# Reordering the products of an MLP's up stage, and preparing two attention weights one stage earlier

## The chip, the core and the metric

The kernel runs on one core of a Trainium2 chip. The metric is the device time of one execution in microseconds (us), and the time of a kernel is the median of its runs. Three runs of the kernel before are known: 2131.23, 2133.43 and 2618.16 us, median 2133.43 us. One more execution was taken with the hardware profiler; it took 2129.71 us.

## What is computed

A two-layer decoder trunk on 1024 tokens of width 1024, in float32:

```python
h = x @ conv_w_in + b;  h = a * sigmoid(gate);  h = depthwise_conv31(h)     # layer 0, token mixer
y = silu(layer_norm(h)) @ conv_w_out + b
...
q = rope(x @ attn_w_q);  k = rope(x @ kv_w_k);  v = x @ kv_w_v               # layer 1, token mixer
y = softmax_with_sink(q k^T in a window of 128) v @ attn_w_o
...
x = layer_norm(ALPHA * x + y)                                               # then, in both layers:
x = layer_norm(ALPHA * x + square(relu(x @ w_up)) @ w_down)                 # MLP, inner width 4096
x = x + (p @ ple_w_proj) * sigmoid(x @ ple_w_gate)                          # gate
```

`w_q` and `w_o` are 1024 x 1024, `w_up` and `w_down` 1024 x 4096 and 4096 x 1024.

## The kernel before, in words

**Three products for one.** Every float32 operand of a matmul is split into a high part, rounded to the fast format, and a low part, the rest. ScalarE (ACT) writes the high part with a cast, VectorE (DVE) the low part with a subtraction (`split`), and TensorE (PE) adds high x high, high x low and low x high (`mm3`). A 128-row step of a 512-column product is thus three matmuls.

**Low parts made ahead.** For some weights the low part is made one stage early, written to DRAM and only loaded when it is needed. `unit_ahead` does this for one unit of `w_q` or `w_o`, a tile of 128 x 1024. For each of its two halves it loads 128 x 512 (256 KB) into a tile with a given tag, casts it into a second tile of that tag, subtracts, and stores the low half to DRAM (`low_half`). That is two loads, two casts, two subtractions and two stores for a unit. `w_q` has eight units, `w_o` is given four here. The consumer later loads the weight itself and its low part with `prep(ap, low=...)`. `work(what, k, tag)` is the call that records one unit, with a priority 400 places later than its place in the program (`LOW_BY`).

**The up stage** (`mlp`, lines 1335 to 1426) takes the 32 column blocks of `w_up` in 16 pairs, f = 0, 2, ..., 30. Each pair is computed as a 2 x 2 block product with seven products in place of eight; a product here is 12 matmuls of 128 x 512. `top_left(f)` makes two of them, into one bank of PSUM and a second one, and its sum gives the first result c11. Then come the products with the four token forms T[2], T[3], T[1] and T[4], and one with the plain tokens `plain[1, 1]`. The running bank p of `top_left` takes T[2], is copied by ACT (c21), takes T[1], is copied (c22), takes `plain[1, 1]` and becomes c12. A second bank r takes T[3] and then T[4]; it is added to c22 between the two and to c21 after T[4]. For the five pairs in `EARLY` = 0, 2, 4, 6, 8 `top_left` runs ahead of the loop. `keep` sums and stores the results. The weights come through a stream `ws` of five slots in the order in which `ws.add` is given them.

**The down stage** (`down_seven`) goes through the eight blocks of the inner width in five groups, `DOWN` = (0), (1, 2), (3, 4), (5, 6), (7). A group makes seven products. In a group of two blocks a product is 48 matmuls into four banks; DVE adds each bank to the output x. The forms of the operands alternate between quarters of the token buffers. In the third group the residual is added as well: 16 loads and 16 DVE operations (`residual`). `product` notes the last matmul ahead of its own as `mark`; the residual loads may start after it (`nc.after(mark)`).

**The gate and the attention.** `ple(0)` computes the gate of layer 0. After its sixth set of products it records eight `work` units for `w_q`, with tag X. Then `attention` makes keys and values (the KV part, with `w_kv`); at the first of its two token groups it records four units for `w_o`, with tag X. The queries follow.

**What sets the order.** A recording layer (`Recorder`) notes every operation, and `schedule` lays them out on the engines with a list scheduler: on each engine the operation that is ready goes first, the smaller priority first, by costs that are written into `cost`. `nc.slack` adds a time in ns to the moment at which the operations recorded under it count as ready: `WORK_SLACK` 1000, `UP_SLACK` 2000. The order is fixed when the program is built; on the chip each engine and the DMA queue of SyncE (SP) run theirs strictly one after the other. All loads and stores are issued by SP. All operations carry line 479, where the recorded calls are made, so the rows of the profile are told apart by tile names: X and z are tags of general tiles, `ps` and `tr` are banks of PSUM, `xh`/`xl` are token buffers or forms, `wh`/`wl` weight slots, `t`, `g`, `bo`, A, B and E general tiles.

Of the kernel before, what the change touches and what calls it, by code (L numbers as in the profile page):

```python
# [16 lines left out]
T = 1024  # L17
# [46 lines left out]
EARLY = 0, 2, 4, 6, 8  # L64
# [4 lines left out]
WORK_SLACK = 1000.0  # L69
UP_SLACK = 2000.0  # L70
# [441 lines left out]
class Emit:  # L512
# [822 lines left out]
    def mlp(self, i):  # L1335
        nc, d, ws = self.nc, self.d, self.ws
        tags, xtags = (dict(zip((2, 1, 3, 4), "XAEB")), "EB") if i == 0 else (dict(zip((2, 1, 3, 4), "XEAB")), "AB")
        pairs = list(range(0, NFF, 2))
        units = {}
        for f in pairs:  # L1340
            u = self.low.get((i, f)) or self.pair_units([d["w_up"][i, f + k] for k in range(2)], f in EARLY)
            units[f] = u if len(u) == 4 else u + self.pair_units([d["w_up"][i, f + k] for k in range(2)], True)[1:]
        ws.add(*[units[f][0] for f in EARLY])
        for f in pairs:
            ws.add(*units[f][f in EARLY :])

        plain = {
            (a, h): [self.xs(k + 4 * a, h * HT, HT) for k in range(4)]
            for a, h in ((0, 0), (1, 0), (1, 1))
        }  # L1350

        def prod(u, half, B, ps=None):
            wh, wl = u
            o = half * HT
            more = ps is not None
            ps = ps if more else self.ps()
            self.mm3(ps, [
                (wh[:, o + k * P : o + (k + 1) * P], wl[:, o + k * P : o + (k + 1) * P], *B[k]) for k in range(4)
            ], not more, True, more)
            return ps  # L1360

        def copy(ps, tag="t"):
            v = self.sb(tag)
            nc.scalar.copy(v, ps)
            return v

        def plus(a, ps):
            nc.vector.tensor_tensor(out=a, in0=a, in1=ps, op=ALU.add)
            return a

        def top_left(f):
            w = ws.get(1)[0]
            p = prod(w, 0, plain[0, 0])
            c = copy(p)
            p2 = prod(w, 1, plain[1, 0])
            ws.done(1)
            return p, self.square(plus(c, p2))

        for k in range(3):
            nc.move("tr", "ps")  # L1380
        banks = {}
        for f in EARLY:
            banks[f], c = top_left(f)
            self.store(i, f, (0, 0), c)
        T = self.token_forms(tags)
        self.quiet = nc.tile("xh01", (P, 4, HT), F32), nc.tile("xl01", (P, 4, HT), F32R)
        self.seven_forms(f"gate{i}", 4)
        self.seven_forms(f"down{i}", 2)

        for f in pairs:  # L1390
            early = f in banks
            if early:
                p, c11 = banks[f], self.sb("t")
                o = f % 4 // 2 * HT
                nc.sync.dma_start(c11, self.hid[i][f // 4, (0, 0)][:, o : o + HT])
            else:
                p, c11 = top_left(f)
            w12 = ws.get(1)[0]
            prod(w12, 0, T[2], p)
            c21 = copy(p)  # L1400
            w34 = ws.get(1)[0]
            r = prod(w34, 0, T[3])
            prod(w12, 1, T[1], p)
            ws.done(1)
            c22 = copy(p, "bo")
            self.square(plus(c22, r))
            w = ws.get(1)[0]
            prod(w34, 1, plain[1, 1], p)
            c12 = self.square(p, "z")
            prod(w, 0, T[4], r)  # L1410
            ws.done(2)
            self.square(plus(c21, r))
            self.keep(i, f, {(0, 0): c11, (0, 1): c12, (1, 0): c21, (1, 1): c22}, early)
            nc.slack = UP_SLACK
            if f in UP_WORK:
                self.work(UP_WORK[f][0] + str(i), UP_WORK[f][1], "Q")
            nc.slack = 0.0
            if f == MARKED:
                self.mark = nc.ops[-1]

        self.x = []
        for t in range(NT):
            self.x.append(self.pair(xtags[t // 4]))
        self.begun = set()
        self.turn = 0
        for n, cs in enumerate(DOWN):
            self.down_seven(i, cs, n == 0, n == len(DOWN) - 1, list(range(NT)) if n == RES else [])

# [52 lines left out]
    def down_seven(self, i, cs, start, end, rest):  # L1481
# [6 lines left out]
        nc, d = self.nc, self.d  # L1488
        sub, add = ALU.subtract, ALU.add
        n = len(cs)  # L1490
# [32 lines left out]
        def product(a, b, to, bank=None, own=(None, None), last=False, low=None, full=()):  # L1523
            f = [[self.form(v, t, l) for v, t, l in zip(p, own, (None, low and made[low][1]))] for p in zip(a, b)]
            new = bank is None
            bank = [self.ps() for t in range(4)] if new else bank
            if last and to == [(0, 1)]:
                for k in range(3):
                    nc.move("ps", "tr")
            for t in range(4):  # L1530
                for k in range(n):
                    self.part(bank[t], *f[k], t, new and k == 0, k == n - 1, not new)
                for h, q in to:
                    self.add_to(t + 4 * h, q, bank[t], sums if (h, q) in full else None)
            for t in range(4 if last else 0):
                with nc.later(LATE if to == [(0, 1)] else 0):
                    self.layer_norm(t + 4 * to[0][0], gb, None, self.raw, sums[t + 4 * to[0][0]])
            mark = [o for o in nc.ops if o.eng == "tensor"][-1 - 24 * n]
            for k in range(2):
                if rest:  # L1540
                    t = rest.pop(0)
                    self.residual(i, t, tags[t % 2], mark)
            return bank

        def first(j, ap):
# [6 lines left out]
        if start:  # L1552
            c = cs[0]
            early = self.xT_quarter((0, 1), F32)
# [53 lines left out]
    def ple(self, i):  # L1608
# [4 lines left out]
        nc, d, ws = self.nc, self.d, self.ws  # L1613
# [54 lines left out]
        p, r, spots = [], [], []  # L1668
# [47 lines left out]
            finish(t + 4, 1, c)  # L1716
        ws.done(2)
        if i == 0:
            nc.slack = WORK_SLACK
            for k in range(8):  # L1720
                self.work("w_q", k, "X")
            nc.slack = 0.0
            self.xT[0, 1] = self.xT_quarter((0, 1))
            for k in range(2):
                nc.move("ps", "tr")
            self.phases_to_xT(1)
# [27 lines left out]
    def attention(self):  # L1754
        nc, d, ws = self.nc, self.d, self.ws
# [19 lines left out]
        ws.pump()  # L1775
        nc.move("raw", "mid")
        for tg in (range(4, 8), range(0, 4)):
            nc.slack = WORK_SLACK
            for k in range(4 if tg[0] else 0):
                self.work("w_o", k, "X")  # L1780
            nc.slack = 0.0
            for ps, t in zip(self.tok_group(tg, us), tg):
                nc.scalar.copy(vf[t // 2][:, t % 2 * 256 : (t % 2 + 1) * 256], ps[:, 256:512])
                kf = self.sb("t")[:, 0:256]
                self.rope(ps[:, 0:256], kf, t, 4)

                pt = self.transpose4([kf[:, j * P : (j + 1) * P] for j in range(2)])
                cols = slice(t % 4 * P, (t % 4 + 1) * P)
                for g in range(4):
                    hi, lo = (kT[g, t // 4][r, cols] for r in ROWS)  # L1790
                    src = pt[ROWS[g % 2], g // 2 * P : (g // 2 + 1) * P]
                    nc.scalar.copy(hi, src)
                    nc.vector.tensor_tensor(out=lo, in0=src, in1=hi.bitcast(F32), op=ALU.subtract)
                if t in (3, 4):
                    for g in range(4):
                        nc.scalar.copy(k34[:, g, t - 3, :], kT[g, t // 4][:, cols].bitcast(F32))
# [7 lines left out]
        for gp in range(2):  # L1804
            us = ws.get(4)
            for n in range(NT):
# [22 lines left out]
                for gl in range(2):  # L1829
# [4 lines left out]
                    p = self.scores(n, 2 * gp + gl, qf[gl])  # L1834
# [259 lines left out]
```

## Time and profile before

| what | value |
|---|---|
| median of three runs | 2133.43 us |
| profiled execution: its own time | 2129.71 us |
| its span, from first to last instruction | 2128.0 us |
| granted TensorE clock | full in all 40 slices |
| TensorE busy | 2111.0 us, 99% |
| VectorE busy | 1696.3 us, 80% |
| ScalarE busy | 1239.3 us, 58% |
| DMA, mean over the span | 218 GB/s |

The stages lie, in us from the span's start: convolution up to about 380, the first up stage about 430 to 704, the first down stage about 704 to 1000, the first gate about 1000 to 1074, the rest of the gate with keys and values about 1074 to 1160, queries and attention about 1160 to 1340, and the second layer's MLP and gate to the end. In the down stage the chain of work shows the groups starting at 742.7 and 818.9 us. A row of a view that carries "<-" behind a time names what ended an idle time. In the table by stretches, each engine has its busy us and its count of instructions, and after them stand the granted clock, the mean busy share of the 16 DMA engines, and GB/s.

### The profile page before, as it was taken

What the parts mean: (1) busy time and instruction counts of PE and PEld (TensorE: products, weight loads), DVE (VectorE), ACT (ScalarE), POOL (GpSimd) and SP (SyncE); (2) the same over time, 40 slices, a digit from 0 to 9 for tenths busy, and PEclk for the clock granted to TensorE, in tenths of its full rate; (3) what the DMA queues carried; (4) which work ended last, traced back from release to release, by engine and by line L of the source; (5) the groups of instructions that cost most, each with busy time, mean ns of one, the idle gap of its engine ahead of it and who ended that gap; (6) DMA issues with size and microseconds to landing.
All of it is one profiled execution on the core that took longest, in us unless ns stands there. A gap on an engine that the chain in (4) does not pass through costs nothing.

```text
span 2128.0 us, 29691 instructions
## 1 busy us (share of the span) xinstructions
PE 2111.0 (99%) x9984; PEld 1748.6 (82%) x9984; DVE 1696.3 (80%) x2750; ACT 1239.3 (58%) x2309; POOL 280.1 (13%) x494
## 2 busy tenths in 40 slices
PE   9999999999999999999999999999999999999998
PEld 7888888878888888888787888888888888888877
DVE  8767698978776879876975888699887778888688
ACT  6655654766666533335756889457666663333484
POOL 0000024100000000001421666150000000000042
PEclk9999999999999999999999999999999999999999
DMA  7778954877778747565486022777877785565726
GB/s 255 230 217 281 284 203 155 293 249 268 264 244 258 271 162 227 193 193 183 164 306 224 22 79 83 220 239 255 284 270 261 265 304 176 178 229 171 258 88 219
DMA packets 219609, 464.00 MB, mean 218 GB/s; under 512 B 22080, under 2 KB 55488, under 8 KB 219456
## 3 DMA queue, kind: packets, MB, share of 16 engines
q1 hardware_dynamic: 219456, 462.11, 65.3%
q8 instruction: 78, 1.28, 0.3%
q14 instruction: 75, 0.61, 0.1%
HBM read 314.96 MB, written 147.06 MB: 217 GB/s over the span
## 4 chain that ended last, share of the span: by engine, by line
PE 86%; DVE 4%; ACT 4%; DMA 3%; issue 1%; POOL 1%; SPq 0%; ACTq 0%; POOLq 0%; DVEq 0%
PE ps L479 67%; PE tr L479 18%; ACT z L479 2%; DMA raw<-in_w_up_dram 1%; DVE wl L479 1%; DVE g L479 1%; POOL sm L479 1%; DVE t L479 1%; ACT wh L479 1%; ACT xh L479 1%; ACT t L479 1%; DVE B L479 0%; DMA raw<-in_w_kv_dram 0%; DMA down_low_t<-xl 0%; DVE X L479 0%
## 5 line engine op out<-in xcount | busy, mean ns | idle before, releaser
L479 PE MATMUL ps<-xh,xl 128*128 128x512 f32 x618 | 240.4, 389 | 0.0
L479 PE MATMUL ps<-xl,xh 128*128 128x512 f32 x618 | 240.4, 389 | 0.0
L479 PE MATMUL ps<-xh 128*128 128x512 f32 x618 | 240.4, 389 | 0.0
L479 POOL TENSOR_SCALAR sm<-sm 128x1 f32<-128x1 f32 x72 | 27.0, 379 | 1371.3 <-DVE E L479 610.7
L479 ACT CAST wh<-raw 128x1024 fp32r<-128x1024 f32 (+2 forms) x156 | 142.1, 915 | 105.6 <-PE ps L479 43.5
L479 PE MATMUL ps<-wh,xh 128*128 128x512 f32 (+1 forms) x460 | 182.9, 398 | 2.4 <-DVE t L479 1.5
L479 PE MATMUL ps<-xh,wh 128*128 128x512 f32 x472 | 183.9, 393 | 1.1 <-ACT bo L479 0.4
L479 PE MATMUL ps<-xl,wh 128*128 128x512 f32 x472 | 184.6, 392 | 0.0
L479 PE MATMUL ps<-xh,wl 128*128 128x512 f32 x472 | 184.1, 390 | 0.0
L479 PE MATMUL ps<-wl,xh 128*128 128x512 f32 (+1 forms) x460 | 183.3, 398 | 0.3 <-DMA wl<-gate_low_t 0.3
L479 PE MATMUL ps<-wh,xl 128*128 128x512 f32 (+1 forms) x460 | 182.7, 397 | 0.0
L479 DVE TENSOR_TENSOR wl<-raw,wh 128x1024 fp32r<-128x1024 f32 (+2 forms) x100 | 98.1, 983 | 59.8 <-ACT wh L479 59.4
L479 ACT CAST xh<-wh 128x1024 fp32r<-128x1024 f32 x76 | 79.7, 1049 | 111.8 <-PE ps L479 89.3
L479 ACT CAST wh<-g 128x512 fp32r<-128x512 f32 x136 | 80.9, 620 | 109.0 <-PE ps L479 66.7
L479 PEld LDWEIGHTS ps<-xh 128*128 128x128 f32 x618 | 116.0, 188 | 24.2
L479 PEld LDWEIGHTS ps<-xh,xl 128*128 128x128 f32 x618 | 116.1, 188 | 24.0
L479 PEld LDWEIGHTS ps<-xl,xh 128*128 128x128 f32 x618 | 116.0, 188 | 24.0
L479 DVE TENSOR_TENSOR wl<-g,wh 128x512 fp32r<-128x512 f32 x136 | 89.4, 685 | 35.3 <-ACT wh L479 35.2
L479 ACT ACTIVATE t<-t 128x512 f32<-128x512 f32 x144 | 91.0, 632 | 31.1 <-DVE t L479 29.2
L479 DVE TENSOR_TENSOR xl<-wh,xh 128x1024 fp32r<-128x1024 f32 x76 | 92.7, 1219 | 20.4 <-ACT xh L479 20.4
L479 PEld LDWEIGHTS ps<-xh,wh 128*128 128x128 f32 x472 | 88.8, 188 | 21.1 <-ACT bo L479 0.8
L479 PEld LDWEIGHTS ps<-xh,wl 128*128 128x128 f32 x472 | 88.8, 188 | 18.5
(425 smaller groups left out, 5623.5 us busy)
## 6 DMA issues: line engine op xcount, KB each, us to landing
wh<-hid SPq DMA_DIRECT2D x78, 512.0 KB, 4.2
raw<-in_w_up_dram SPq DMA_DIRECT2D x68, 512.0 KB, 4.2
wl<-in_w_down_dram SPq DMA_DIRECT2D x58, 512.0 KB, 4.8
hid<-zz SPq DMA_DIRECT2D x96, 256.0 KB, 4.7
z<-in_w_dw_dram SPq DMA_DIRECT2D x64, 288.0 KB, 4.3
hid<-t SPq DMA_DIRECT2D x64, 256.0 KB, 4.5
raw<-hid SPq DMA_DIRECT2D x30, 512.0 KB, 3.9
hid<-z SPq DMA_DIRECT2D x36, 256.0 KB, 4.7
```

Of the source, the lines that this page charges most:

```text
L479: getattr(getattr(nc, o.eng), o.name)(*a, **k)
```

## The change

It has two parts.

**In the up stage of both layers**, the inner loop runs in another order. For the pairs that aren't early, `top_left(f + 2)` is computed inside pair f, between the product with T[3] and the one with T[4]; the weight stream is reordered to match. T[4] now comes before T[1]. r is therefore copied by ACT after T[3] (c22), before T[4] is added to it, and p is added to c22 after T[1].

**In the first layer**, the eight units of `w_q` and the four of `w_o` are no longer recorded behind the gate and in the KV part. They are put on a list, `self.ahead`, and one is recorded at the end of each of the first twelve products of the two-block groups of the down stage, with tag z in place of X, with `UP_SLACK` in place of `WORK_SLACK`, and with its operations held back until the product's `mark`.

```diff
         for f in pairs:
-            ws.add(*units[f][f in EARLY :])
+            ws.add(*units[f][1:3])
+            if f + 2 in pairs and f + 2 not in EARLY:
+                ws.add(units[f + 2][0])
+            ws.add(units[f][3])
...
         for f in pairs:
-            early = f in banks
+            early = f in EARLY
+            p = banks[f]
             if early:
-                p, c11 = banks[f], self.sb("t")
+                c11 = self.sb("t")
                 o = f % 4 // 2 * HT
                 nc.sync.dma_start(c11, self.hid[i][f // 4, (0, 0)][:, o : o + HT])
             else:
-                p, c11 = top_left(f)
+                c11 = ready
             w12 = ws.get(1)[0]
             prod(w12, 0, T[2], p)
             c21 = copy(p)
             w34 = ws.get(1)[0]
             r = prod(w34, 0, T[3])
+            c22 = copy(r, "bo")
+            if f + 2 in pairs and f + 2 not in EARLY:
+                banks[f + 2], ready = top_left(f + 2)
+            w = ws.get(1)[0]
+            prod(w, 0, T[4], r)
+            ws.done(1)
+            self.square(plus(c21, r))
             prod(w12, 1, T[1], p)
             ws.done(1)
-            c22 = copy(p, "bo")
-            self.square(plus(c22, r))
-            w = ws.get(1)[0]
+            self.square(plus(c22, p))
             prod(w34, 1, plain[1, 1], p)
+            ws.done(1)
             c12 = self.square(p, "z")
-            prod(w, 0, T[4], r)
-            ws.done(2)
-            self.square(plus(c21, r))
...
+        self.ahead = [] if i else [(w, k) for w, n in (("w_q", 8), ("w_o", 4)) for k in range(n)]
         for n, cs in enumerate(DOWN):
             self.down_seven(i, cs, n == 0, n == len(DOWN) - 1, list(range(NT)) if n == RES else [])
...
                     self.residual(i, t, tags[t % 2], mark)
+            if len(cs) == 2 and self.ahead:
+                nc.slack = UP_SLACK
+                with nc.after(mark):
+                    self.work(*self.ahead.pop(0), "z")
+                nc.slack = 0.0
             return bank
...
         if i == 0:
-            nc.slack = WORK_SLACK
-            for k in range(8):
-                self.work("w_q", k, "X")
-            nc.slack = 0.0
             self.xT[0, 1] = self.xT_quarter((0, 1))
...
         for tg in (range(4, 8), range(0, 4)):
-            nc.slack = WORK_SLACK
-            for k in range(4 if tg[0] else 0):
-                self.work("w_o", k, "X")
-            nc.slack = 0.0
             for ps, t in zip(self.tok_group(tg, us), tg):
```

## The prediction

> **What bounds the kernel now.** I read the page first, then who PE waited for, then a table of busy time by stage.
>
> ```profile
> span 2128.0 us, 29691 instructions
> PE 2111.0 (99%) x9984; PEld 1748.6 (82%) x9984; DVE 1696.3 (80%) x2750; ACT 1239.3 (58%) x2309; POOL 280.1 (13%) x494
> PEclk9999999999999999999999999999999999999999
> PE 86%; DVE 4%; ACT 4%; DMA 3%; issue 1%; POOL 1%; SPq 0%; ACTq 0%; POOLq 0%; DVEq 0%
> ```
>
> PE is busy for 2111.0 of 2128.0 us at the full clock, so it is idle for only 17.0 us. The change leaves the count and the size of the matmuls as they are. What can be won is therefore a part of those 17.0 us, under 1%. What can be lost has no such bound. A busy PE can still be slow, so I take its pace from the chain of work:
>
> ```profile
> 742.70 5.44 PE tr L479 x24
> ```
>
> Twenty-four matmuls in 5.44 us are 0.2267 us each, in the down stage. The stages that the change touches:
>
> ```profile
> 430.00:700.00 270.00, 268.77 (x1181) 220.58 (x1180) 201.79 (x313) 167.04 (x285) 0.00 (x0) 1.00 0.79 263
> 742.00:904.00 162.00, 162.00 (x717) 134.13 (x716) 135.54 (x170) 57.83 (x67) 0.00 (x0) 1.00 0.59 194
> 1000.00:1074.00 74.00, 71.79 (x343) 58.20 (x342) 67.04 (x114) 54.29 (x98) 28.72 (x28) 1.00 0.42 141
> 1074.00:1160.00 86.00, 83.83 (x408) 68.41 (x407) 59.01 (x131) 52.64 (x123) 12.83 (x13) 1.00 0.87 299
> 1480.00:1720.00 240.00, 239.89 (x1058) 197.88 (x1057) 185.34 (x288) 152.56 (x259) 0.00 (x0) 1.00 0.81 270
> ```
>
> The columns are PE, its weight loads, DVE, ACT, POOL, the clock, DMA share and GB/s. PE is idle for 1.23 us in the first up stage, 0 in the down stage's middle, 2.21 in the first gate, 2.17 in the rest of the gate and KV, and 0.11 in the second up stage. That is 5.7 us in all, and none of it in the place to which the work moves.
>
> **Part 1, the up stage.** No matmul is added. One ACT copy reads r in place of p, and DVE adds p to it. What can move is the waits; these are the first up stage's:
>
> ```profile
> PE ps L479 <- ACT t L479: 0.7, 2, 0.5
> PE ps L479 <- ACT bo L479: 0.4, 1, 0.4
> ```
>
> The longest one, in order of time:
>
> ```profile
> 440.31 0.39 PE L479 MATMUL ps<-E,wl 128*128 128x512 f32 x1
> 440.59 0.58 ACT L479 COPY t<-ps 128x512 f32<-128x512 f32 x1
> 441.22 0.72 PE L479 MATMUL ps<-A,wh 128*128 128x512 f32 x2 [0.52 <-ACT t L479]
> 441.26 0.63 ACT L479 CAST wh<-g 128x512 fp32r<-128x512 f32 x1
> ```
>
> T[1] (tile A) waits for the copy of p, because ACT began it late; T[3] (tile E), 12 x 0.2267 = 2.72 us, was its cover. In the changed program's order, pairs from the fifth on have T[3], 24 matmuls of the next pair, and T[4] behind the copy, 48 x 0.2267 = 10.9 us, so this wait goes there. In the first four pairs no next `top_left` is left to insert. There the order is T[3], five matmuls of T[1], T[4], the rest of T[1]: the old wait stays, and T[4] gets a new one, for the copy of r behind only 5 x 0.2267 = 1.13 us. The copy needs 0.58 us and the hand-offs in the rows about 0.05 at each side, so 0.68 us: it fits, unless ACT is in a full-width cast when r ends, 1.05 us:
>
> ```profile
> L479 ACT CAST xh<-wl 128x1024 fp32r<-128x1024 f32 x22 | 23.1, 1050 | 1.0 <-DVE wl L479 1.0
> ```
>
> Then 0.68 + 1.05 - 1.13 = 0.6 us is lost, at most in four pairs of two layers, 4.8 us. The gain is at most 1.2 us. I take -0.5 for waits that go and +0.5 for new ones: 0 in all, ends -1.2 and +4.8. Weight slots and raw tiles keep their count; the next pair's first load comes one unit earlier, which the 0.79 DMA share carries as before.
>
> **Part 2, what leaves the gate and KV.** Twelve units: 24 loads, 24 casts, 24 subtractions, 24 stores.
>
> ```profile
> L479 ACT CAST X<-X x24: 614/622/632, 1081.3 to 1156.0; 128x512 fp32r<-128x512 f32 x24
> L479 DVE TENSOR_TENSOR X<-X,X x24: 676/688/1775, 1090.0 to 1157.5; 128x512 fp32r<-128x512 f32 x24
> L479 SPq DMA_DIRECT2D X<-in_w_q_dram x16: 332/333/512, 1074.4 to 1124.9; - x16
> L479 DVE TENSOR_TENSOR X<-X,X 128x512 fp32r<-128x512 f32 x24 | 17.9, 760 | 9.0 <-ACT X L479 8.8
> ```
>
> They start at 1074.4 us, so the 2.21 us of idle PE before that (layer-norm and gate waits) aren't theirs, and I take nothing from it. From 1074 to 1160 they put 17.9 us on DVE, 14.4 us (24 x about 0.62, less overlap) on ACT and 12.6 MB (48 x 256 KB) on DMA, of 86 x 299 = 25.7 MB. PE's waits there:
>
> ```profile
> PE ps L479 <- DVE B L479: 0.9, 2, 0.6
> PE ps L479 <- DVE xl L479: 0.8, 1, 0.8
> PE ps L479 <- POOL t L479: 0.4, 1, 0.4
> ```
>
> They add up to 2.1 us, near the 2.17 of idle PE. One of them seen from DVE:
>
> ```profile
> 1148.89 0.68 DVE L479 TENSOR_TENSOR X<-X,X 128x512 fp32r<-128x512 f32 x1
> 1150.81 1.54 DVE L479 TENSOR_TENSOR B<-ps,B 64x128 fp32r<-64x128 f32 x6
> 1151.98 0.41 PE L479 MATMUL ps<-ident,t 128*128 128x128 f32 x2 [0.57 <-DVE B L479]
> ```
>
> One 0.68 us subtraction of this work stands on DVE shortly ahead of the key operations (tile B) whose late end holds PE for 0.57 us. Without it they'd end earlier by up to that. The wait for `xl` falls before the first of these subtractions (1090.0), and only the ACT casts (from 1081.3) can have a part in it. I take -1.5, ends 0 and -2.2. Nothing new is late: the low parts are then in DRAM some 190 us before they are first loaded, and the loads of `w_kv` and `w_q` behind them on SP's queue move up.
>
> **Part 3, what comes into the down stage.** The units stand at twelve products of 48 x 0.2267 = 10.9 us, from about 742 to 873 us, and drain to about 904. Each end of a residual or of a form on DVE costs as follows here:
>
> ```profile
> L479 DVE TENSOR_TENSOR xl<-t,xh 128x512 fp32r<-128x512 f32 x8 | 5.4, 686 | 0.7 <-ACT xh L479 0.7
> L479 ACT CAST xh<-t 128x512 fp32r<-128x512 f32 x8 | 4.8, 617 | 13.0 <-PE ps L479 13.0
> 834.98 1.22 DVE L479 TENSOR_TENSOR xl<-wl,xh 128x1024 fp32r<-128x1024 f32 x1
> 836.11 0.68 DVE L479 TENSOR_TENSOR E<-E,ps 128x512 f32<-128x512 f32 x1
> 839.33 0.39 PE L479 MATMUL ps<-xl,xh 128*128 128x512 f32 x1
> 818.00:860.00 42.00, 42.00 (x187) 34.76 (x186) 41.93 (x56) 14.84 (x19) 0.00 (x0) 1.00 0.82 277
> ```
>
> DVE gets 24 x 0.686 = 16.5 us onto 135.54 of 162: 152, it still fits. ACT gets 24 x 0.617 = 14.8 us onto 57.83: free. But from 818 to 860 DVE is already full (41.93 of 42), with the residuals. The closest hand-off I find there: the form that starts at 834.98 ends at 836.20, and PE first reads it at 839.33, so 3.1 us are left (that it is the same form follows from the buffer numbers in the program's order). In the changed order three of the subtractions fall between the first and the last residual, 3 x 0.69 = 2.1 us; the others stand outside. 2.1 is below 3.1, so I cost DVE at nothing; its cover gone, each product of that group would start late by what is over.
>
> DMA is tighter. A unit moves 1.05 MB per product, 1.05 / 10.9 = 96 GB/s:
>
> ```profile
> 818.00:873.00 55.00, 55.00 (x244) 45.54 (x243) 51.43 (x69) 20.48 (x25) 0.00 (x0) 1.00 0.73 246
> 840.00:860.00 20.00, 20.00 (x90) 16.56 (x89) 19.97 (x28) 6.72 (x11) 0.00 (x0) 1.00 0.95 328
> 960.00:980.00 20.00, 20.00 (x90) 16.57 (x89) 12.16 (x20) 11.72 (x17) 0.00 (x0) 1.00 0.98 358
> SPq L479 <- DVE xl L479: 118.0, 49, 8.1
> ```
>
> The most that a 20 us stretch shows is 358 GB/s, at a share of 0.98. From 818 to 873 the sum is 246 + 96 = 342, just below; from 840 to 860 it is 328 + 96 = 424, over by 66 GB/s for 20 us, 1.3 MB, which at 358 GB/s is 3.7 us of lateness. SP waited 118.0 us for forms to free weight slots, so loads are issued as a slot comes free, and a queue with 48 more entries puts each added wait (for PE's mark, a subtraction in z, a free z tile) in front of the loads of weights and of the inner activations behind it, for which DVE's forms and then PE wait. POOL runs nothing from 742 to 904 and none of the moved work. PE has 0 us of waits there now, and I take +0.5, ends 0 and +3.7.
>
> Against those 358 stands a page of the Trainium skill. HBM Reference, section Specifications (TRN2), says that a core streaming alone measures well above the paired-core share of about 358 GB/s, at about 425. By that figure the 424 just fits and the lateness is 0 in place of 3.7 us; no row of this trace goes above 358 over 20 us, so the row decides the end of my range.
>
> **The sum.** 0 - 1.5 + 0.5 = -1 us on the profiled execution's 2129.71, with ends -1.2 - 2.2 = -3.4 and +4.8 + 3.7 = +8.5. The known undisturbed times are 2129.71, 2131.23 and 2133.43; the median given, 2133.43, is 3.7 above the profile. I set -1 against the middle one: 2130 us.
>
> **Rivals.**
> - *Faster than I say*: with less on DVE, ACT and DMA all idle PE of the touched stages goes, 5.7 us, to about 2125. For it: DVE is at 67.04 of 74 us in the gate. Against: 2.21 us of it fall before the moved work begins.
> - *Slower: late loads in the third down group.* The point from which it decides is where a load's lateness passes its cover: 3.7 us against a DVE cover of 3.1 us. If it passes and SP's queue doesn't catch up, each of the five products that still carry units starts late by about 2 us: +10, to about 2141. For it: the share of 0.95, and SP in strict order. Against: 873 to 904 has room again (a mean of 194 GB/s over the whole stretch). Only if all twelve products lost 3.7 us, 44 us, would it be over 2%.
> - *Slower: the copy of r holds T[4]* in the eight early pairs: +4.8, to about 2136. Against: ACT is at 167.04 of 270 us, so a long cast is seldom in the way.
> - *It doesn't do what it says*: KV's waits are DVE's own chain of small key operations, and nothing changes, 2131.
>
> **How the numbers follow.** The forecast and "nothing changes" can't be told apart and have 0.68 together. Faster, 2125, has 0.11; late loads 0.12, of which 0.03 for over 2%; the copy of r 0.08; 0.01 is left for a gain over 2%, which 17.0 us of idle PE all but exclude. The range goes from 2123 (2129.71 less 5.7, rounded down) to 2144 (2133.43 plus 10). A measurement of this kernel tells about 2%, 43 us, from no change; that gives faster 0.01, same 0.96, slower 0.03.
>
> **What would show it.** PE's busy time stays near 2111 and the span near 2127. Between 1074 and 1160 PE's idle time falls from 2.17 to below 1 and DMA from 299 GB/s to about 150. From 742 to 904 DMA rises to about 270 GB/s, DVE to about 152 us, PE's idle time stays below 1. In the up stage, waits for `t` remain only in the first four pairs. I am wrong if PE waits for forms (`xl`) between 818 and 904, or if T[4] waits for `bo`.

## The result and the profile after

The changed kernel takes 2138.12 us (median of 12 runs, 2135.67 to 2143.34), the kernel before 2131.81 us beside it. The ratio is 1.0031, with a 95% interval of 1.0022 to 1.0039: slower by 0.31%, 6.6 us, where a gain of about 1 us was forecast. The profiled execution took 2136.92 us. One of the 12 known runs of the kernel before (2618.16 us) was disturbed and is left out of the ratio.

From the page of the changed kernel:

```profile
span 2135.2 us, 29618 instructions
PE 2113.9 (99%) x9984; PEld 1748.6 (82%) x9984; DVE 1694.5 (79%) x2752; ACT 1242.6 (58%) x2309; POOL 276.8 (13%) x492
PE 79%; DMA 7%; DVE 6%; ACT 4%; issue 2%; POOL 1%; SPq 1%; DVEq 0%; ACTq 0%; POOLq 0%
```

PE still does 9984 matmuls. Its busy time grew by 2.9 us with the same work, so some of them were slow, and its idle time grew from 17.0 to 21.3 us. In the chain of work, the last of these lines, PE has 79% in place of 86% and DMA 7% in place of 3%: more of the chain now runs through a wait and the load behind it. The table by stages says where; first the changed kernel, then the one row of the kernel before that is new here:

```profile
430.00:704.00 274.00, 271.05 (x1180) 221.54 (x1179) 201.61 (x314) 168.02 (x285) 0.00 (x0) 0.99 0.75 259
742.00:904.00 162.00, 162.00 (x716) 134.16 (x715) 147.59 (x190) 70.11 (x89) 0.00 (x0) 1.00 0.79 268
840.00:860.00 20.00, 20.00 (x90) 16.57 (x89) 17.42 (x24) 7.26 (x11) 0.00 (x0) 1.00 0.82 280
1074.00:1160.00 86.00, 83.82 (x406) 68.48 (x405) 43.06 (x109) 41.17 (x98) 8.16 (x7) 1.00 0.52 167
1480.00:1720.00 240.00, 237.52 (x1039) 194.19 (x1038) 183.34 (x285) 151.21 (x255) 0.00 (x0) 1.00 0.77 260
```

```profile
430.00:704.00 274.00, 272.77 (x1198) 223.89 (x1197) 205.33 (x318) 170.05 (x289) 0.00 (x0) 1.00 0.79 265
```

The count behind PE's busy time is the better measure here, because it also shows slow matmuls. In the same 274 us of the first up stage PE gets 18 matmuls less done (1180 against 1198), in 240 us of the second 19 less (1039 against 1058). At 0.2267 us each that is 4.1 and 4.3 us. The down stage, which took in the work, lost nothing, and the gate and KV, which gave it away, won nothing (83.82 against 83.83 us of PE). In this one execution the up stage also began 2.2 us earlier, behind the convolution, which the change does not touch: the 2200th matmul starts at 423.85 us against 426.03. The 8.4 us of the two up stages less these 2.2 are 6.2 us; most of the rest of the 7.2 us between the spans lies in the attention (1160 to 1340 us), where PE is busy for 178.34 us against 179.37.

PE's waits in the changed kernel, in the first up stage (430 to 704 us) and then in the second (1470 to 1730 us):

```profile
PE ps L479 <- ACT bo L479: 1.8, 1, 1.8
PE ps L479 <- DVE bo L479: 0.5, 1, 0.5
PE tr L479 <- DVE bo L479: 0.4, 1, 0.4
```

```profile
PE ps L479 <- DVE v L479: 1.2, 2, 1.0
PE ps L479 <- DVE z L479: 0.9, 2, 0.7
PE ps L479 <- ACT z L479: 0.7, 1, 0.7
```

The waits for `t` and `bo` that the prediction showed are gone. There are two new kinds. The first is T[4] (tile B) waiting for ACT's copy of r, in the first pair of each layer: 1.85 us in the first (the tile is `bo`) and 0.65 us in the second (z):

```profile
1476.93 0.73 PE L479 MATMUL ps<-B,wh 128*128 128x512 f32 x2 [0.65 <-ACT z L479]
```

The second is the product with the plain tokens waiting for DVE's addition of p to c22 (the tile is `bo` in the first layer, v or z in the second). The first kind in the first layer, as PE and then ACT and DVE show it in the timeline of the changed kernel:

```profile
439.05 0.61 PE L479 MATMUL ps<-A,wh 128*128 128x512 f32 x2
441.51 0.73 PE L479 MATMUL ps<-B,wh 128*128 128x512 f32 x2 [1.85 <-ACT bo L479]
```

```profile
438.64 1.82 ACT L479 CAST wh<-g 128x512 fp32r<-128x512 f32 x3 [2.20 <-DVE g L479]
440.37 0.61 ACT L479 CAST xl<-xh 128x512 fp32r<-128x512 f32 x1
440.88 0.58 ACT L479 COPY bo<-ps 128x512 f32<-128x512 f32 x1
```

```profile
437.91 0.69 DVE L479 TENSOR_TENSOR g<-raw 128x512 f32<-128x512 f32 x1 [4.42 <-DMA raw<-in_w_up_dram]
```

Read them from below. A load of `w_up` landed late, and DVE stood idle for 4.42 us for it. ACT stood behind DVE for 2.20 us. Then ACT had three casts of the weight and one of a form, 2.4 us in its strict order, ahead of the copy of r. PE had five matmuls of T[1], 1.13 us, to hide all that.

Right behind this wait comes, in the profiled execution, what raised PE's busy time:

```profile
438.80:442.20 3.40, 1.55 (x7) 0.97 (x6) 3.40 (x7) 3.18 (x6) 0.00 (x0) 1.00 0.66 203
442.20:445.60 3.40, 3.40 (x10) 2.62 (x9) 3.03 (x6) 0.62 (x1) 0.00 (x0) 0.50 0.59 155
```

```profile
443.28 0.63 PE L479 MATMUL ps<-B,wl 128*128 128x512 f32 x1
443.71 1.05 PE L479 MATMUL ps<-B,wh 128*128 128x512 f32 x2
444.56 0.63 PE L479 MATMUL ps<-B,wl 128*128 128x512 f32 x1
```

The granted clock is 0.50 for 3.4 us. Three matmuls take from 443.28 to 444.56 us, 0.427 us each instead of 0.2267, so eight are done in the time of fifteen: 7 x 0.2267 = 1.6 us lost while PE counts as busy.

Most executions don't have this stretch. Half of 3.413 us in a span of 2135.2 us takes 0.08% off the mean clock, and this run is on record with 0.999. Of the 12 runs of the changed kernel only three have 0.999, at 2136.92 (this one), 2137.85 and 2140.18 us, on both sides of the median; the other nine have 1.0. So at most three had such a stretch. It belongs to the profiled execution and doesn't explain the median.

The second kind of wait, all engines, in the second layer (E is T[1] there, X the next pair's T[2], and `xh` the plain product):

```profile
1565.94 0.39 PE L479 MATMUL ps<-E,wl 128*128 128x512 f32 x1
1566.55 1.22 DVE L479 TENSOR_TENSOR wl<-raw,wh 128x1024 fp32r<-128x1024 f32 x1
1566.85 0.61 PE L479 MATMUL ps<-X,wh 128*128 128x512 f32 x2
1567.69 0.68 DVE L479 TENSOR_TENSOR v<-v,ps 128x512 f32<-128x512 f32 x1
1568.42 0.50 PE L479 MATMUL ps<-xh,wh 128*128 128x512 f32 x1 [0.96 <-DVE v L479]
```

p is ready when T[1] ends, at about 1566.3. DVE is then in a full-width subtraction of 1.22 us, adds p at 1567.69, and the five matmuls of X are over before it is done. Before the change an ACT copy of 0.58 us released p at this place. A wait costs more than its listed length: behind this one the second matmul starts 0.34 us after the first (1568.42 and 1568.76), in place of 0.2267.

### The profile page after: what moved, and what is told of

Its sections match the earlier page's. It is cut to its first block, busy times and chain, and to the rows that moved or that the text cites. A ratio compares the mean times of both kernels' runs of the same rounds, so it can differ in the third digit from the quotient of the medians.

```text
span 2135.2 us, 29618 instructions
## 1 busy us (share of the span) xinstructions
PE 2113.9 (99%) x9984; PEld 1748.6 (82%) x9984; DVE 1694.5 (79%) x2752; ACT 1242.6 (58%) x2309; POOL 276.8 (13%) x492
## 4 chain that ended last, share of the span: by engine, by line
PE 79%; DMA 7%; DVE 6%; ACT 4%; issue 2%; POOL 1%; SPq 1%; DVEq 0%; ACTq 0%; POOLq 0%
PE ps L479 63%; PE tr L479 16%; DMA raw<-in_w_up_dram 2%; ACT z L479 2%; DMA hid<-zz 1%; DVE wl L479 1%; DVE g L479 1%; DVE xl L479 1%; POOL sm L479 1%; DMA t<-proj 1%; DVE t L479 1%; DVE zz L479 1%; ACT wh L479 1%; DVE z L479 1%; SPq L479 1%
## 5 line engine op out<-in xcount | busy, mean ns | idle before, releaser
L479 PE MATMUL ps<-xh 128*128 128x512 f32 x654 | 254.4, 389 | 0.0
L479 PE MATMUL ps<-xl,xh 128*128 128x512 f32 x654 | 254.4, 389 | 0.0
L479 PE MATMUL ps<-xh,xl 128*128 128x512 f32 x654 | 254.4, 389 | 0.0
L479 PE MATMUL ps<-wh,xh 128*128 128x512 f32 (+1 forms) x432 | 170.2, 395 | 2.6 <-DVE t L479 1.5
L479 PE MATMUL ps<-wl,xh 128*128 128x512 f32 (+1 forms) x432 | 171.0, 396 | 0.2 <-DMA wl<-gate_low_t 0.2
L479 PE MATMUL ps<-wh,xl 128*128 128x512 f32 (+1 forms) x432 | 170.9, 396 | 0.0
L479 PEld LDWEIGHTS ps<-xl,xh 128*128 128x128 f32 x654 | 122.8, 188 | 25.6
L479 ACT CAST xh<-wh 128x1024 fp32r<-128x1024 f32 x76 | 79.7, 1049 | 90.9 <-PE ps L479 66.8
L479 DVE TENSOR_TENSOR wl<-raw,wh 128x512 fp32r<-128x512 f32 (+2 forms) x100 | 97.2, 974 | 21.5 <-ACT wh L479 20.0
L479 DVE TENSOR_TENSOR t<-t,ps 128x512 f32<-128x512 f32 (+1 forms) x143 | 81.0, 567 | 40.7 <-PE ps L479 24.4
L479 PEld LDWEIGHTS ps<-xl,wh 128*128 128x128 f32 x472 | 88.6, 188 | 18.7 <-DVE xl L479 1.6
```

The lines of the kernel that those rows point to most:

```text
L479: getattr(getattr(nc, o.eng), o.name)(*a, **k)
```

## The experiments

Theory A: the loss is made by these two hand-offs, the copy of r ahead of T[4] in the first four pairs, and DVE's addition of p ahead of the plain product. Rival B: the moved work makes it, by filling DVE and DMA in the down stage. Two more rivals came up on the way: C, that the early wait is all there is, and D, that this wait is an accident of one execution. Besides, PSUM banks held for longer were a third view for e3_swap.

| kernel | median us | ratio to before, 95% | matmuls in 430 to 704 / 1480 to 1720 |
|---|---|---|---|
| before | 2131.8 | | 1198 / 1058 |
| changed | 2138.12 | 1.0031, 1.0022 to 1.0039 | 1180 / 1039 |
| e1_part1 | 2136.54 | 1.0025, 1.0016 to 1.0034 | 1192 / 1045 |
| e2_part2 | 2133.19 | 1.0007, 0.9998 to 1.0016 | 1199 / 1051 |
| e3_swap | 2130.72 | 0.9997, 0.9988 to 1.0006 | 1203 / 1049 |
| e4_copy | 2141.11 | 1.0049, 1.0037 to 1.0062 | 1180 / 1046 |
| e5_early_swap | 2135.39 | 1.0010, 1.0002 to 1.0019 | 1195 / 1045 |
| e6_late_swap | 2133.60 | 1.0004, 0.9995 to 1.0013 | 1196 / 1049 |
| e7_swap_only | 2131.28 | 0.9993, 0.9984 to 1.0001 | 1204 / 1050 |
| e8_two_copies | 2137.01 | 1.0023, 1.0014 to 1.0032 | 1191 / 1040 |

The stages lie a few us apart in these executions, so a count is good to some matmuls only. The kernel before was run again beside the others: 2131.83 us beside e1 to e4, 2132.72 us beside e5 to e8. So the ratios compare across the rows, the medians only roughly. e9_again (2140.46 us) and e10_doses (2142.17 us) are single executions, without an interval, beside one of 2130.36 us of the kernel before. The planner lays out all engines anew for each version, so two versions differ in more than the lines of the edit.

**One part at a time.** e1_part1 has the new up loop and leaves the units where they were. e2_part2 has the moved units and the old loop.

> The new up loop alone; the twelve units of w_q and w_o stay behind the gate and in the KV part. Theory A (the up loop made two new waits on PE: T[4] for the copy of r, the plain product for DVE's addition of p): about 2138 us, ratio to before 1.003, PE idle in the first up stage about 3 us and in the second about 2.5 us, as after. Rival B (the moved work costs the time): about 2131 us, ratio 1.000.

> The moved units alone, with the up loop of before. Theory A: 2130 to 2132 us, ratio 0.999 to 1.000, PE idle in the up stages 1.2 and 0.1 us as before. Rival B: about 2138 us.

The up loop alone costs 0.25%, the moved work 0.07% with an interval that holds zero, and together they come to about the 0.31% of the whole. Rival B falls. PE idles 2.3 and 1.5 us in the two up stages of e1_part1 (about 3 and 2.5 expected) and 1.4 and 1.1 us in those of e2_part2 (1.2 and 0.1 expected). So about 1 us of idle time in the second up stage, and 7 matmuls (1051 against 1058), come and go between executions of the old loop. e2_part2 also answers what part 2 was worth. PE's waits and the row of its gate and KV:

```profile
PE ps L479 <- DVE xl L479: 1.1, 1, 1.1
PE ps L479 <- DVE B L479: 0.9, 1, 0.9
```

```profile
1074.00:1160.00 86.00, 83.89 (x412) 68.73 (x410) 42.96 (x111) 41.31 (x99) 9.51 (x12) 1.00 0.51 162
```

DVE's load there fell from 59.01 to 42.96 us and DMA's from 299 to 162 GB/s, and PE is idle for the same 2.1 us: the wait for B is 0.9 us as before, the one for `xl` grew from 0.8 to 1.1, and the one for `t` went.

**The order of T[1] and T[4].**

```diff
+            prod(w12, 1, T[1], p)
+            ws.done(1)
+            self.square(plus(c22, p))
             w = ws.get(1)[0]
             prod(w, 0, T[4], r)
             ws.done(1)
             self.square(plus(c21, r))
-            prod(w12, 1, T[1], p)
-            ws.done(1)
-            self.square(plus(c22, p))
             prod(w34, 1, plain[1, 1], p)
```

> The whole change, but T[1] stands before T[4] in every pair: 12 matmuls (2.7 us) lie between T[3] and T[4] in the early pairs, and T[4] (2.7 us) between T[1] and the plain product. Theory A: both new waits get a cover; 2129 to 2132 us, PE idle below 1.2 us in either up stage. Rival B: 2138 us. A third view, that top_left in the middle of a pair costs PSUM banks: PE idle stays about 3 and 2.5 us and the time about 2137.

Three lines moved take the loss away: 0.9997 against 1.0031. The same matmuls, copies and additions run, and the moved work is there too. What the edit changes is the cover: the copy of r now has all of T[1] behind it, and the addition of p all of T[4]. In the first up stage 1203 matmuls fit (1180 before the swap), and no wait for `bo` is left:

```profile
PE ps L479 <- ACT t L479: 0.9, 1, 0.9
```

In the second up stage 1049 matmuls fit (1039 before the swap; 1051 in e2_part2 with the old loop). But PE idles 1.76 us there, above the 1.2 us expected, and the plain product still waits for DVE's addition:

```profile
PE ps L479 <- DVE v L479: 1.2, 1, 1.2
PE ps L479 <- DVE z L479: 0.5, 1, 0.5
```

The longer of the two, DVE and then PE:

```profile
1558.52 0.69 DVE L479 TENSOR_TENSOR zz<-z,z 128x512 f32<-128x512 f32 x1 [2.75 <-DMA hid<-zz]
1562.13 0.68 DVE L479 TENSOR_TENSOR v<-v,ps 128x512 f32<-128x512 f32 x1
1562.87 0.50 PE L479 MATMUL ps<-xh,wh 128*128 128x512 f32 x1 [1.20 <-DVE v L479]
```

DVE stood idle for a late load of `hid` and then had six operations, 3.6 us from the first start to the addition of p. That is more than the 2.72 us of T[4]. A whole product of cover made the second hand-off cheaper and did not close it.

The view that the banks of PSUM are held for longer falls with this: the swap holds r for longer than the change does, by T[1], and the loss is gone.

**The engine of the second hand-off.** Here ACT copies p, and DVE adds the copy.

```diff
-            self.square(plus(c22, p))
+            self.square(plus(c22, copy(p)))
```

> The whole change, but DVE's addition no longer reads the bank p: ACT copies p into a tile first, as before the change, and DVE adds the copy. Theory A: the plain product no longer waits for DVE; the second up stage's PE idle falls from 2.5 to below 1 us, the wait of T[4] for the copy of r in the early pairs stays; 2133 to 2136 us. Rival B: 2138 us.

The expectation missed: 0.49% slower than before, worse than the change. It was not DVE as such. In the first up stage of e4_copy (PE does six matmuls of X, the next pair's T[2], between T[1] and the plain product):

```profile
610.19 1.29 ACT L479 ACTIVATE t<-t 128x512 f32<-128x512 f32 x2 [2.19 <-DVE t L479]
611.39 0.60 ACT L479 CAST wh<-raw 128x512 fp32r<-128x512 f32 x1
611.90 0.58 ACT L479 COPY t<-ps 128x512 f32<-128x512 f32 x1
612.53 0.50 PE L479 MATMUL ps<-xh,wh 128*128 128x512 f32 x1 [1.32 <-ACT t L479]
```

ACT too has 1.9 us of other work standing ahead of the copy at that moment, at a mean load of 59%. On either engine five or six matmuls (1.13 or 1.36 us) are too little cover. The longest wait of that stage is another, though: T[1] waits 1.53 us at 456.13 us for the copy of p behind T[2]. That the third copy in a pair is the reason is likely and not shown.

**The two hand-offs apart.** e5_early_swap puts T[1] ahead of T[4] in the first four pairs alone (`if f + 2 in EARLY:`), e6_late_swap in the others alone.

> The whole change, with T[1] ahead of T[4] only in the first four pairs (f = 0 to 6), where no top_left stands between T[3] and T[4]. The later pairs stay as changed. Theory A (two hand-offs, each with its own cost) expects the copy of r to cost nothing here: the wait of 1.85 us at 441.5 goes and with it the stretch at half clock, 3.4 us together, and the plain product's waits in the later pairs stay (1.4 us in the first layer, 2.7 in the second): about 2138.1 - 3.5 = 2134.6 us. Rival C (the early wait is all there is, and what the whole swap won over the change in the later pairs is noise) expects about 2131. Rival D (the later pairs are all that matters in every run, the half clock is an accident of one profile) expects about 2137.

> The whole change, with T[1] ahead of T[4] only from f = 8 on. The first four pairs stay as changed. Theory A expects the plain product's waits to go from the later pairs (4.1 us of them in the profile, about 1.2 of which the kernel before had elsewhere) and the wait for the copy of r with its half clock to stay: 2138.1 - 3.5 = 2134.6 us. Rival C expects 2138, rival D about 2132. The two savings of this run and of e5 should add up to the 7.4 us that the swap in all pairs saved.

Both gain and neither gains all: against the change's 0.31%, e5 takes off 0.21 and e6 0.27 (each good to some 0.12). That is 4.5 and 5.8 us, where about 3.5 us each were expected. Rival C expected 2131 us for e5 and 2138 for e6, rival D 2137 for e5; the intervals exclude all three. The late pairs' waits do stay in e5 and the early wait stays in e6. The sum of the two savings is above the swap's 0.34, which the errors allow. In e6's profile the early wait also came out shorter, 0.40 us instead of 1.85, with no half clock behind it. Its order on ACT is the same:

```profile
438.52 1.83 ACT L479 CAST wh<-g 128x512 fp32r<-128x512 f32 x3 [0.74 <-DVE g L479]
440.25 0.62 ACT L479 CAST xl<-xh 128x512 fp32r<-128x512 f32 x1
440.77 0.58 ACT L479 COPY bo<-ps 128x512 f32<-128x512 f32 x1
```

Only ACT's idle time ahead of the casts differs. Over the runs, ACT's idle time and PE's wait go together: 2.20 and 1.85 us in the changed kernel, 1.84 and 1.49 in e1_part1, 0.74 and 0.40 here, always 0.35 apart. In this order on ACT the wait is the lateness of one weight load, passed on in full.

**The copy doubled, and the change once more.** e8_two_copies:

```diff
+            if f + 2 in EARLY:
+                copy(r)
             c22 = copy(r, "bo")
```

> The whole change, with the copy of r made twice in the first four pairs, first into an unused tile: ACT holds r for 0.58 us longer ahead of T[4], behind the same five matmuls of T[1]. Theory A expects waits of T[4] in all the early pairs: 0.68 + 0.58 - 1.13 = 0.13 us at least in each, with a long cast ahead 1.2 us and more, so up to 0.6 us more in each of eight pairs, 4.8 us in all: 2139 to 2143 us, and more stretches at half clock where a wait comes near 1.9 us (about 1.7 us each). Whoever holds the copy for harmless (rivals B and D) expects 2138.

> The changed kernel once more, unchanged, for one look: does the wait of T[4] for the copy of r at about 441 us come back at its length of 1.85 us, and the 3.4 us at half clock behind it? If both belong to the program (theory A), a wait of 1.5 to 1.9 us stands there again; a half clock only if it is above 1.5 us, the longest wait that the other profiles show without one. If the wait is set by when a load lands (rival D: an accident of one execution), it comes back below 0.5 us, as the 0.40 us of e6_late_swap, whose early pairs are those of the change.

e8 missed: 2137.01 us, not more than the change. With the second copy the planner ordered ACT anew, ACT's idle time was 0.38 us and T[4] waited 0.33 us. Only one of the first layer's early pairs shows the wait, and two of the second's (0.51 and 0.20 us). Order and lateness changed together with the copy, so this run doesn't tell what the copy's length alone costs. e9, the change itself, shows the wait again at 444.56 us:

```profile
441.69 1.82 ACT L479 CAST wh<-g 128x512 fp32r<-128x512 f32 x3 [2.14 <-DVE g L479]
```

```profile
444.56 0.74 PE L479 MATMUL ps<-B,wh 128*128 128x512 f32 x2 [1.79 <-ACT bo L479]
```

```profile
446.10:449.50 3.40, 3.40 (x10) 2.66 (x9) 2.82 (x6) 0.62 (x1) 0.00 (x0) 0.50 0.90 254
```

The wait is 1.79 us (again 0.35 below ACT's idle time), and the half clock came with it. In both profiles of this program the wait is there, so it is no accident of one. The half clock needs more than the program: nine of the 12 runs went without it.

**The swapped order without the moved work.** e7_swap_only is e3_swap with the units in their old places.

> The swapped order in all pairs, as in e3_swap, but without the moved work: the units of w_q and w_o are made behind the gate and in the KV part, as in the kernel before. If the moved work costs what e2_part2 measured (+0.07%, 1.4 us) this is about 2129.3 us, the fastest version so far; if it costs nothing, 2130.7 as e3_swap; if it is worth the 1.5 us that the prediction gave it, 2132.2.

2131.28 us, 0.9993 with an interval of 0.9984 to 1.0001: the lowest ratio of all versions, and still not told apart from the kernel before, nor from e3_swap. Also with a whole product behind both hand-offs, the new order of the up stage brought no gain that the measurement can show. PE still waits in its second up stage for DVE's addition of p, twice for 0.9 us.

**Waits of several lengths, for the clock.** e10_doses copies p up to nine times more in five pairs (`for k in range({0: 6, 2: 7, 4: 8, 6: 9, 30: 7}.get(f, 0)): copy(p)`).

> The order of e7_swap_only, with p copied by ACT 6, 7, 8 and 9 times more (into unused tiles) in the first four pairs and 7 times more in the last one, of both layers: T[1] can start only when the last of these copies has read p, so PE gets waits of several lengths where no other product is at hand. For the clock: if an idle time of about 1.9 us is enough for a stretch at half clock, each wait above that is followed by one of 3.4 us, and none below 1.5 us is; if the half clock in the changed kernel had another cause, waits of 2 us and more stand here without one. The copies alone are 37 x 0.58 = 21 us of ACT for each layer; the time is 2131 us plus whatever part of it PE waits for, at most 21 us in each layer.

One execution, 2142.17 us. The planner filled most of the room that the copies made, so only two waits are long enough to tell something:

```profile
441.91 0.50 PE L479 MATMUL ps<-X,wh 128*128 128x512 f32 x1 [1.56 <-ACT wh L479]
1755.14 0.50 PE L479 MATMUL ps<-xl,xh 128*128 128x512 f32 x1 [2.03 <-DVE xl L479]
```

The shorter one was followed by the half clock, at 443.4 us, and the longer one was not. So the expectation missed on both, and length alone does not decide; the last section takes this up.

## Why the prediction was wrong

**Part 1 is the step that failed**: "0 in all, ends -1.2 and +4.8". Alone it measures 0.25% of 2131.8, 5.3 us (3.4 to 7.2). Three things are in that.
- The old waits went in the changed kernel's profile (0.7 + 0.4 us in the first up stage), in the first four pairs too, where the prediction kept one. In e1_part1 one of 0.55 us for `t` stands at 694.80 us, in the last pair: it has no next `top_left` to insert either, and the prediction counted only the first four pairs as such.
- T[4]'s wait for the copy of r was seen as a mechanism, down to the five matmuls of cover, and mis-sized. Its price was "ACT is in a full-width cast when r ends, 1.05 us", so 0.6 us. In the profiled execution ACT had four casts of 0.61 us ahead of the copy, three of them set free together by one late load: 1.85 us, and 1.6 us more for the half clock behind it. The wait came in the first pair of each layer, not in four. The reason against it, that ACT is busy for only 167.04 of 270 us, is where the thought went wrong. A mean load says how often an engine is busy, not how much stands ahead of one instruction when a late load releases several at once.
- The plain product's wait for DVE's addition of p was not in the sum at all. The change swaps an ACT copy for a DVE addition as the operation that releases p, and only r's side was costed. It makes 0.9 us of listed waits in the first up stage and 2.1 us in the second, where the kernel before had 0.11 us of idle PE (e2_part2, with the same loop, 1.1). Who reads p last, and what comes next on that engine, was to be asked for both accumulators.

By e5_early_swap and e6_late_swap the order costs time in the early and in the late pairs, some 0.2 to 0.3% each with errors of 0.12. How the 5.3 us of the median divide between the two hand-offs stays open.

**Part 2, -1.5 us, did not come**: e2_part2 shows 1.0007 and the same 2.1 us of idle PE. In e1_part1, with the units in the old places, PE idles only 0.93 us in that stretch, so its idle time moves by more than 1 us without them. The step that failed is the reading of one row, a 0.68 us subtraction a little ahead of the key operations, as their cause. DVE in the changed kernel, where no such subtraction is left, and then PE:

```profile
1129.33 0.61 DVE L479 TENSOR_TENSOR B<-ps,B 64x128 fp32r<-64x128 f32 x2
1129.97 0.23 DVE L479 TENSOR_TENSOR t<-zz 128x64 f32<-128x64 f32 x1
1130.23 0.29 DVE L479 TENSOR_TENSOR B<-tr,B 64x128 fp32r<-64x128 f32 x1
1130.55 0.61 DVE L479 TENSOR_TENSOR B<-ps,B 64x128 fp32r<-64x128 f32 x2
```

```profile
1131.31 0.41 PE L479 MATMUL ps<-ident,t 128*128 128x128 f32 x2 [0.88 <-DVE B L479]
```

DVE runs the key operations back to back, and PE waits 0.88 us for them. That is the fourth rival's mechanism, "DVE's own chain of small key operations", and for this wait it was right. DVE's load fell by a quarter (59.01 to 43.06 us), and its 32 key operations kept their 0.29 us each. What makes the wait for `xl`, 0.8 us before and 1.1 after, stays open.

**Part 3 was right**, +0.5 forecast and 0 in the trace: no idle PE in 162 us, no wait for `xl`, DMA at 268 GB/s (about 270 forecast), DVE at 147.59 us (152). Between 840 and 860 us DMA moved 280 GB/s, not the 424 that the sum asked for. So the clash on which the 3.7 us hung did not occur, and the figure of about 425 GB/s alone (the Trainium skill, HBM Reference, Specifications (TRN2)) was not put to the test by it.

**The rivals.** The closest was "the copy of r holds T[4]", 2136 us, given 0.08. The place was right; the size was near by chance, since one long wait in each layer and the uncosted plain product took the place of eight short waits. The mark "wrong if T[4] waits for `bo`" is the one that showed it.

## What to carry to other kernels

When an accumulator is read out between two products, cost the hand-off by the queue that can stand ahead of the read-out when the slowest load of that stage lands, not by the reader's mean load, and give it a whole product of cover where one is at hand. A late load can outlast even that, as the 1.20 us in e3_swap show. Swapping two products that do not depend on each other won back 0.34% here at no other cost that was measured. And taking load off an engine can shorten a wait only if that load stands inside the chain that PE waits for; look for it there, instruction by instruction.

## What the runs showed of the hardware

In the up stage a single idle time of 1.85, 1.79 or 1.56 us of PE (the change, its second profile, e10_doses; one execution each) was followed by 3.413 us at half clock, which costs 1.6 us more. The records of the granted clock change only at whole multiples of 3.413 us from the first one, and each of these three waits lies within one such stretch; the half clock starts with the next. In the same stage e1_part1's wait of 1.49 us was followed by full clock. The 2.03 us wait of e10_doses, also followed by full clock, lies across a boundary, some 1.0 us on each side, and so does e4_copy's of 1.53 us (1.33 and 0.20). One row does not fit a plain limit between 1.49 and 1.56 us, nor the 1.5 us that the expectation for e9_again took for the longest wait without a half clock. It stands in e1_part1, in the attention:

```profile
1236.08 0.70 PE L479 MATMUL ps<-A,v 128*128 128x512 f32 x2 [1.70 <-DVE t L479]
```

It lies within one stretch, by the multiples, and full clock followed. Whether the kind of matmul beside the wait counts, or the edges are a little off, stays open.

The Trainium skill, TensorE: Matmul & The Clock Gate, Part 1 (the HAM clock gate), gives a free-running window of 3413 ns, and the traces agree: the half clock lasted 3.413 us. A table there puts the half rate behind at least one idle window of about 3.4 us. The measurement differs: waits of about half that length were enough in three profiles, and by the page's rule none of these kernels would have lost the 1.6 us.
